# A two-layer fp32 trunk on one core: left operands two products ahead in the value stage, row scaling on ScalarE, reloads in pieces, another share of projection and output steps

## The chip, the cores and the metric

The kernel runs on one core of one Trainium2 chip. The metric is the device time of one execution in microseconds, lower being better. TensorE (PE) multiplies; VectorE (DVE), ScalarE (ACT) and GpSimd (POOL) work on tiles of 128 partitions; SyncE (SP) issues the DMAs. Each engine runs its own instructions in order and waits on semaphores for the others.

## The reference, cut to what matters

```python
def reference(x, ...):                       # x: 1 x 2048 x 1024, float32
    h = rms_norm(x, a_norm_g[0])             # layer 0: chunked gMLP
    x = x + gmlp_mixer(h, a_w_in[0], ...)
    k_pad, v_pad = shared_kv(x, kv_norm_g, w_kv)   # rms_norm(x) @ w_kv, once
    h = rms_norm(x, b_norm_g[0])             # layer 1: band attention
    x = x + chunk_attention_mixer(h, k_pad, v_pad, b_w_qz[0], b_rel_bias[0], b_w_out[0])
    return rms_norm(x, final_norm_g)
```

The attention has 16 heads of 64 channels. Each chunk of 64 rows attends to itself and the eight chunks before it, with a relative-position bias, and the result is gated by silu(z) before the output projection. All of it is float32.

## The kernel before, in words

Float32 accuracy comes from three matmuls: each operand is split into a rounded high part and the rest (hi, lo), and `mm3` (lines 113 to 115) adds hi by hi, hi by lo and lo by hi into one PSUM bank. A split is a cast on ACT followed by a subtraction on DVE. The large matrix products use a form of Strassen's scheme: seven products of half-size blocks in place of eight, the sums of blocks being formed on POOL and DVE. The 2048 rows go in four row tiles t of 512, each of four blocks b of 128 rows.

The kernel has three stages. The first, to about 1349 us of the span, is the gMLP layer; it leaves x in DRAM (`x1d`). The second is the **value stage** (the `with` block from line 1085), to 1549 us. The third is attention with its projections and the output projection.

The value stage computes v = rms_norm(x) @ w_v with `strassen("vp{t}", ...)` for each t. There are 14 products per t: the phases `PHS = (1, 7, 2, 6, 5, 4, 3)`, each for two row halves jp. Each product is four steps k of `mm3`, 12 matmuls of 128x512. `strassen` is a generator that yields after every step, so that other work can be put between. At step k = 1 of product i it calls `ready(i + 1)`, which splits the left operand of the next product: `split_s` casts into Shv on ACT (line 269) and subtracts into Slv on DVE (line 270); the tiles are in a ring "S" of eight buffers. `left` then forms the next block sums on POOL in place (lines 1112 to 1117). At the same point `weigh` calls `right` for a phase to come, with `look` saying how far: at t = 0 this loads and splits that phase's weights (line 186 on ACT, 187 on DVE). `evict` takes the finished PSUM bank (four of them): products of phases 1 and 7 are copied by ACT into vu (line 1148), the others are added by DVE (1153 to 1164), and finished parts are split again into v on ACT (1135) and DVE (1136) and stored.

Between the products of tile t the loop at the end of the stage prepares tile t + 1. At yields 1, 4, 7 and 10 `norm(t + 1, b)` loads a block of x, squares it with a row sum on ACT (line 133), takes the power -1/2 in `root` (an addition on DVE, line 126, and the power on POOL, line 127) and scales the rows on DVE (line 138). At yields 20, 28, 36 and 44 `block(t + 1, b)` transposes the block on PE (line 153), copies it back on ACT (157) and stores it (158) for later. For t = 1 and 2 the pieces of `o_sums` form block sums of the output weights on POOL, split them into tiles of the same ring "S" and store them. At t = 3, yield 20, `reload(0)` reads the four transposed blocks of tile 0 back (line 164), casts them into `hh` (167, ACT) and subtracts into `hl` (168, DVE). hh and hl have one buffer each.

The attention stage goes over t and, within it, eight head pairs p. For each pair the loop of eight u does: scores two units ahead (`score`: matmul line 1302, bias and row maximum on DVE 1310, exponential on ACT 1317, reciprocal on DVE 1320, scaling on POOL 1321), transposes of the probabilities (`flip`: PE 1341, copies on ACT 1344, split on DVE 1345) and the product with v (`value`: PE 1362 to 1369). Between them `take(gen, n)` draws steps from a generator `ahead(t, p)`, each step being three matmuls: the projection of the next pair (`project` for q and k, `gate` for z, 8 steps each, lines "pj") and then steps of the output projection of the tile before, `outs[t - 1]` ("bo"), of which `SHARE` says how many go to each pair. `steps_of` counts the steps, and they are spread evenly over 16 slots (two per u). At a **tile border** (p = 7, t < 3) the generator first calls `reload(t + 1)`, then gives 4 bo steps, then the 16 projection steps of the next tile's first pair, then 8 bo steps, spread so that 11 slots would hold them. Ahead of the loops the first pair is projected alone, and of the next pair's projection 4 steps are drawn before each of the first two scores.

## Time and profile before

| | |
|---|---|
| median of three executions | 2731.74 us (2731.46 to 2737.39) |
| the profiled execution | 2731.49 us |
| its span in the profile | 2729.7 us |
| mean granted TensorE clock | 0.987 |
| start of the value stage's matmuls | 1350.0 us |
| start of the attention stage | 1549.0 us |
| busy ACT / POOL | 49% / 33% of the span |

How to read it: the profile is one execution, and all positions are microseconds from the start of its span. "Busy" is the share in which an engine ran an instruction; the granted clock is the TensorE clock that the throttle gave, as a share of full speed. A row of the timeline has start, duration, engine, line of the kernel, operation and operands; brackets hold the idle time of that engine just before it and what ended it. A row of the waits has the engine, the waiting line, the engine or DMA that it waited for, total us, number of times and the longest.

### The profile page before, as it was taken

Reading aid. Unit: us, or ns where it says so; the run is one execution under the profiler, and the core shown is the slowest. Engines: PE = TensorE matmul, PEld = TensorE weight load, DVE = VectorE, ACT = ScalarE, POOL = GpSimd, SP = SyncE. Lnnn points to the kernel's source line nnn. Section 1 sums busy time; section 2 is a strip of 40 time slices with the busy share of each in tenths; the row PEclk is TensorE's granted clock in tenths of the full one; section 3 lists DMA queues with packets and bytes.
Section 4 is the critical chain, followed back from the end, with each engine's and each line's share of the span. In section 5 each row is a group of like instructions: output and inputs, shape, how many; then the busy total and the mean of one; then the engine's idle time right before and its main releaser. Section 6 shows DMA issues by size and latency. Waiting matters only on the chain. (4 is left out here: it accounts for less than half of the span.)

```text
span 2729.7 us, 38869 instructions
## 1 busy us (share of the span) xinstructions
PE 2629.2 (96%) x13216; PEld 2199.6 (81%) x13216; DVE 1970.0 (72%) x3097; ACT 1327.0 (49%) x2360; POOL 907.7 (33%) x906
## 2 busy tenths in 40 slices
PE   8999999999999999999989899899999999999997
PEld 7788888888888888888867677788887888788875
DVE  5655676676666668667677777777778778877787
ACT  5422242433434345332455455656656566656553
POOL 3512226142351314114234444323232223323243
PEclk9999999999999999999989999999999999999999
DMA  8898999989989879678668778766777667866677
GB/s 299 309 332 335 348 353 327 332 299 352 333 301 310 286 269 345 224 244 318 236 221 283 250 249 256 253 207 196 231 247 256 204 220 229 272 197 193 187 227 248
DMA packets 274774, 735.57 MB, mean 269 GB/s; under 512 B 29584, under 2 KB 61328, under 8 KB 274576
## 3 DMA queue, kind: packets, MB, share of 16 engines
q1 hardware_dynamic: 274576, 733.09, 78.3%
q8 instruction: 105, 1.72, 0.2%
q14 instruction: 93, 0.76, 0.1%
HBM read 540.56 MB, written 181.93 MB: 265 GB/s over the span
## 5 line engine op out<-in xcount | busy, mean ns | idle before, releaser
L113 PE MATMUL P<-T,S 128*128 128x512 f32 x1248 | 495.0, 397 | 2.1 <-ACT S L360 2.1
L115 PE MATMUL P<-T,S 128*128 128x512 f32 x1248 | 489.4, 392 | 0.0
L114 PE MATMUL P<-T,S 128*128 128x512 f32 x1248 | 488.1, 391 | 1.1 <-DVE T L363 1.1
L1321 POOL TENSOR_SCALAR pr<-pr,sl 128x640 f32<-128x640 f32 (+4 forms) x256 | 201.9, 789 | 548.1 <-DVE sl L1320 494.6
L113 PE MATMUL pj<-hh_b,wh_b 128*128 128x512 f32 x768 | 316.2, 412 | 6.0 <-ACT wh_b L186 4.2
L1317 ACT ACTIVATE pr<-pr,nm 128x640 f32<-128x640 f32 (+4 forms) x256 | 195.5, 764 | 229.1 <-DVE nm L1310 224.0
L114 PE MATMUL pj<-hl_b,wh_b 128*128 128x512 f32 x768 | 306.2, 399 | 0.0
L115 PE MATMUL pj<-hh_b,wl_b 128*128 128x512 f32 x768 | 305.6, 398 | 0.0
L115 PEld LDWEIGHTS P<-T,S 128*128 128x128 f32 x1248 | 234.8, 188 | 50.1
L113 PEld LDWEIGHTS P<-T,S 128*128 128x128 f32 x1248 | 235.2, 189 | 46.8 <-ACT S L360 2.3
L114 PEld LDWEIGHTS P<-T,S 128*128 128x128 f32 x1248 | 235.2, 188 | 46.6 <-DVE T L363 1.3
L1345 DVE TENSOR_TENSOR pt<-tp,pt 128x640 fp32r<-128x640 f32 (+4 forms) x256 | 188.7, 737 | 74.6 <-ACT pt L1344 72.5
L1310 DVE CUSTOM_DVE_ANT_0 pr<-s,bias 128x640 f32<-128x640 f32 (+4 forms) x256 | 188.1, 735 | 26.0 <-PE s L1302 20.7
L1341 PE MATMUL tp<-ident,pr 128*128 128x128 f32 x1120 | 167.0, 275 | 19.5 <-DVE pt L1345 16.9
L1341 PEld LDWEIGHTS tp<-ident,pr 128*128 128x128 f32 x1120 | 134.8, 141 | 63.2 <-issue 21.4
L1344 ACT CAST pt<-tp 128x640 fp32r<-128x640 f32 (+4 forms) x256 | 158.7, 620 | 52.7 <-PE tp L1341 49.9
L115 PEld LDWEIGHTS pj<-hh_b,wl_b 128*128 128x128 f32 x768 | 146.6, 191 | 32.7
L113 PEld LDWEIGHTS pj<-hh_b,wh_b 128*128 128x128 f32 x768 | 147.5, 192 | 25.7 <-ACT wh_b L186 5.8
L114 PEld LDWEIGHTS pj<-hl_b,wh_b 128*128 128x128 f32 x768 | 147.3, 192 | 16.9
L187 DVE TENSOR_TENSOR wl_b<-raw_b,wh_b 128x1024 fp32r<-128x1024 f32 x96 | 126.6, 1320 | 29.1 <-ACT wh_b L186 28.0
L1369 PE MATMUL pv<-pt,V 128*128 128x256 f32 x960 | 142.4, 288 | 0.9 <-ACT pt L1344 0.9
L1369 PEld LDWEIGHTS pv<-pt,V 128*128 128x128 f32 x960 | 127.0, 193 | 3.1 <-ACT pt L1344 1.8
(291 smaller groups left out, 5952.6 us busy)
## 6 DMA issues: line engine op xcount, KB each, us to landing
S<-hsd SPq DMA_DIRECT2D x288, 512.0 KB, 5.5
rw<-in_w_a SPq DMA_DIRECT2D x108, 512.0 KB, 6.4
A<-ytd SPq DMA_DIRECT2D x72, 512.0 KB, 5.8
raw_b<-wk SPq DMA_DIRECT2D x72, 512.0 KB, 3.9
hsd<-S SPq DMA_DIRECT2D x56, 512.0 KB, 4.4
V<-vhd SPq DMA_DIRECT2D x56, 512.0 KB, 4.7
wh_bo<-ows SPq DMA_DIRECT2D x50, 512.0 KB, 4.4
wl_bo<-ows SPq DMA_DIRECT2D x50, 512.0 KB, 5.6
```

The source lines that it names most:

```text
L113: mm(ps, lh, rh, start=first, stop=False)
L114: mm(ps, lh, rl, start=False, stop=False)
L115: mm(ps, ll, rh, start=False, stop=last)
L187: tv(wl[:], raw[:], wh[:].bitcast(F32), op=sub)
L1310: nc.vector.tensor_tensor_reduce(out=pr[:, c0:].rearrange("p (a b) -> p a b", a=nseg), in0=ps[:, :nseg, :w], in1=bias[:, c0:].rearrange("p ...
L1317: nc.scalar.activation(pr[:, c0:], pr[:, c0:], AF.Exp, scale=-1.0, bias=nm[:], accum_out=sl[:])
L1321: nc.gpsimd.tensor_scalar(pr[:, c0:], pr[:, c0:], sl[:], 1.0, op0=ALU.mult, op1=ALU.mult)
L1341: tpose(tp[:, b, :], pr[:, b * P : (b + 1) * P], ident[:])
L1344: nc.scalar.copy(oh, tp[:, b0:5, :])
L1345: nc.vector.tensor_tensor(pt[:, 1, b0 + qq : 5 + qq, cs], tp[:, b0:5, :], oh.bitcast(F32), op=ALU.subtract)
L1369: mm(po[:, 0, :], keys(i), pt[:, j, i, :], start=(t == 0 and j == 0 and i == blocks[0]), stop=(j == 1 and i == blocks[-1]),)
```

## The change

The change does six things.

- `norm` scales the rows with ScalarE for t = 1 to 3; t = 0 stays on VectorE.
- `strassen` has a new argument `ahead`, the number of products by which left operands are split ahead: 2 in the value stage, 1 in the output projection. In the value stage `look` is 1 for every t, and the weights of phase 2 are loaded and split by `v_weights(2)` ahead of tile 0's products.
- `reload` returns a function of the block. At t = 3 of the value stage the four pieces come at yields 20, 25, 30 and 35; at the borders pieces 0 and 1 come at u = 0 and pieces 2 and 3 at u = 1, ahead of that u's first steps.
- `SHARE` is (2, 7, 7, 7, 7, 7, 7, 12) for every t; before it was (2, 8, 8, 9, 9, 8, 8, 4) for t = 1 and 2 (t = 0 uses none).
- At the borders of t = 1 and 2, 8 bo steps stand ahead of the 16 projection steps and 4 behind them. A new `due` spreads the steps there: two bo steps in each of the first four slots, then 17/8 steps per slot; at t = 0 nothing in the first four slots.
- Ahead of each of the first two scores 6 steps are drawn, not 4.

```diff
--- before.py
+++ after.py
@@ -135,7 +135,10 @@
             accum_out=r[:],
         )
         root(r[:])
-        nc.vector.tensor_scalar(xt[:], xt[:], r[:], None, op0=ALU.mult)
+        if t:
+            nc.scalar.mul(xt[:], xt[:], r[:])
+        else:
+            nc.vector.tensor_scalar(xt[:], xt[:], r[:], None, op0=ALU.mult)
 
     def x_tiles(t):
         th = sh.tile([P, KD, T], F32R, tag="hh", name=f"hh_b{t}")
@@ -159,13 +162,16 @@
 
     def reload(t):
         th, tl = x_tiles(t)
-        for b in range(TB):
+
+        def one(b):
             xt = sh.tile([P, D], F32, tag="raw", name=f"xr_b{t}_{b}", bufs=4)
             nc.sync.dma_start(xt[:], xtd[t][b][:])
             x3 = xt[:].rearrange("p (k c) -> p k c", k=KD)
             oh = th[:, :, b * P : (b + 1) * P]
             nc.scalar.copy(oh, x3)
             tv(tl[:, :, b * P : (b + 1) * P], x3, oh.bitcast(F32), op=sub)
+
+        return one
 
     def scaled(raw, gain):
         k = gain.shape[1]
@@ -231,7 +237,7 @@
 
     PHS = (1, 7, 2, 6, 5, 4, 3)
 
-    def strassen(name, right, left, evict, look):
+    def strassen(name, right, left, evict, look, ahead):
 
         todo = [(ph, jp) for ph in PHS for jp in range(2)]
         rts, views = {}, {}
@@ -246,7 +252,8 @@
                 views[i] = left(*todo[i])
 
         weigh(1)
-        ready(0)
+        for i in range(ahead):
+            ready(i)
         for i, (ph, jp) in enumerate(todo):
             ps = pmm.tile([P, 512], F32, tag="mm", name=f"{name}_{ph}_{jp}")
             vs = views.pop(i)
@@ -256,7 +263,7 @@
                 mm3(ps[:], *vs[k], hi[:, c], lo[:, c], k == 0, k == 3)
                 if k == 1:
                     weigh(i // 2 + (2 if jp else 1 + look))
-                    ready(i + 1)
+                    ready(i + ahead)
                 if k < 3:
                     yield
             evict(ph, jp, ps[:])
@@ -1088,15 +1095,18 @@
             for q in range(2):
                 vw[ph, q] = [vp.tile([P, 1024], F32R, name=f"vw{i}{ph}_{q}")[:] for i in "hl"]
 
+        def v_weights(ph):
+            for q in range(2):
+                if ph in (6, 5):
+                    vw[ph, q] = [w_tile(f"vw{i}{ph}_{q}")[:] for i in "hl"]
+                raw = vp.tile([P, 1024], F32, tag="st", name=f"st{ph}_{q}", bufs=4)
+                nc.sync.dma_start(raw[:], vwf[ph, q][:])
+                split_in(raw, *vw[ph, q])
+
         def v_right(t):
             def right(ph):
-                if t == 0 and ph not in (1, 7):
-                    for q in range(2):
-                        if ph in (6, 5):
-                            vw[ph, q] = [w_tile(f"vw{i}{ph}_{q}")[:] for i in "hl"]
-                        raw = vp.tile([P, 1024], F32, tag="st", name=f"st{ph}_{q}", bufs=4)
-                        nc.sync.dma_start(raw[:], vwf[ph, q][:])
-                        split_in(raw, *vw[ph, q])
+                if t == 0 and ph not in (1, 7, 2):
+                    v_weights(ph)
                 return [vw[ph, q] for q in range(2)]
             return right
 
@@ -1170,15 +1180,19 @@
             vp.tile([P, D], F32, tag="xo", name=f"xo_b{t}_{b}", bufs=4) if t % 2 else even(t, b)
         )
         for t in range(NT):
+            if t == 0:
+                v_weights(2)
             for i, _ in enumerate(
-                strassen(f"vp{t}", v_right(t), v_left(t), v_evict(t), 1 if t else 2)
+                strassen(f"vp{t}", v_right(t), v_left(t), v_evict(t), 1, 2)
             ):
                 if t + 1 < NT and i in (1, 4, 7, 10):
                     norm(t + 1, i // 3, v_junk)
                 if t + 1 < NT and i in (20, 28, 36, 44):
                     block(t + 1, (i - 20) // 8)
                 if t + 1 == NT and i == 20:
-                    reload(0)
+                    again = reload(0)
+                if t + 1 == NT and i in (20, 25, 30, 35):
+                    again((i - 20) // 5)
                 if 0 < t < NT - 1 and i == 4:
                     todo = o_sums(t - 1, lambda n: v_tile("wo", n, 4), lambda n: vp.tile(
                         [P, 512], F32R, tag="S", name=n, bufs=8
@@ -1556,12 +1570,11 @@
 
         def o_all(t):
             yield from strassen(
-                f"bo{t}", o_right(t), o_left(t), o_evict(t), (t + 1) // NT
+                f"bo{t}", o_right(t), o_left(t), o_evict(t), (t + 1) // NT, 1
             )
 
         outs = [o_all(t) for t in range(NT)]
-        SHARE = {t: (2, 8, 8, 9, 9, 8, 8, 4) for t in range(NT)}
-        SHARE[NT - 1] = (2, 7, 7, 7, 7, 7, 7, 12)
+        SHARE = (2, 7, 7, 7, 7, 7, 7, 12)
 
         def take(gen, n):
             for _ in range(n):
@@ -1587,21 +1600,19 @@
                     yield from gate(t, 0)
                 yield from gate(t, p + 1)
                 if t:
-                    yield from some(outs[t - 1], SHARE[t][p])
+                    yield from some(outs[t - 1], SHARE[p])
             else:
-                if t + 1 < NT:
-                    reload(t + 1)
                 if t:
-                    yield from some(outs[t - 1], 4)
+                    yield from some(outs[t - 1], 8)
                 if t + 1 < NT:
                     yield from project(t + 1, 0)
                     values(t + 1, 0)
                 if t:
-                    yield from some(outs[t - 1], 8)
+                    yield from some(outs[t - 1], 4)
 
         def steps_of(t, p):
             n = (32 if p == 0 else 24) if p + 1 < NPAIR else (16 if t + 1 < NT else 0)
-            return n + (SHARE[t][p] if t else 0)
+            return n + (SHARE[p] if t else 0)
 
         load_bias(0, 0)
         gen = project(0, 0)
@@ -1609,16 +1620,24 @@
         values(0, 0)
         first = ahead(0, 0)
         for u in range(2):
-            take(first, 4)
+            take(first, 6)
             score(0, 0, u)
         before = None
         for t in range(NT):
             for p in range(NPAIR):
                 gen = ahead(t, p) if t + p else first
-                total = steps_of(t, p) - (0 if t + p else 8)
+                total = steps_of(t, p) - (0 if t + p else 12)
                 if t + 1 == NT and p + 1 == NPAIR:
                     last_open()
-                per = 11 if p + 1 == NPAIR and t + 1 < NT else 16
+                border = p + 1 == NPAIR and t + 1 < NT
+                if border:
+                    again = reload(t + 1)
+
+                def due(n):
+                    if not border:
+                        return total * (n + 1) // 16
+                    return (8 if t else 0) * min(n + 1, 4) // 4 + max(0, n - 3) * 17 // 8
+
                 todo = []
                 if t == 0 and p in (2, 4):
                     todo = o_sums(p // 2 + 1, lambda n: half_tile("C", n, 4), lambda n: half_tile(
@@ -1630,7 +1649,10 @@
                         score(t, p, u + 2)
                     elif p + 1 < NPAIR or t + 1 < NT:
                         score(t + (p + 1) // NPAIR, (p + 1) % NPAIR, u - 6)
-                    upto = total * (2 * u + 1) // per
+                    if border and u < 2:
+                        again(2 * u)
+                        again(2 * u + 1)
+                    upto = due(2 * u)
                     take(gen, upto - done)
                     done = max(done, upto)
                     flip(t, p, u)
@@ -1643,7 +1665,7 @@
                             value(t, p, *divmod(u // 2 - 1, 2))
                         elif before:
                             value(*before, 1, 1)
-                    upto = total * (2 * u + 2) // per
+                    upto = due(2 * u + 1)
                     take(gen, upto - done)
                     done = max(done, upto)
                 if t + 1 < NT or p + 1 < NPAIR:
```

## The prediction, written before the changed kernel was run

> **What bounds the kernel now.** I read the page's busy shares first, then busy time by window, then TensorE's own timeline with the releasers of its idle time, and last the engines that it waits for.
>
> ```profile
> span 2729.7 us, 38869 instructions
> ...
> PE 2629.2 (96%) x13216; PEld 2199.6 (81%) x13216; DVE 1970.0 (72%) x3097; ACT 1327.0 (49%) x2360; POOL 907.7 (33%) x906
> ```
>
> TensorE is busy 96% of the span, and the change takes no matmul away. So only its idle time, 2729.7 - 2629.2 = 100.5 us, and the time at a lower granted clock can be won. The windows by stage show how much of that lies where the change works. The columns are window, length, PE, PEld, DVE, ACT and POOL busy with counts, granted clock, DMA share and GB/s. Four rows are the row tiles t = 0 to 3 of the value stage, the fifth is the start of attention, three are the tile borders.
>
> ```profile
> 1348.80:1404.00 55.20, 46.21 (x200) 37.50 (x201) 44.44 (x60) 35.72 (x65) 24.39 (x19) 0.91 0.73 258
> 1404.00:1452.40 48.40, 43.83 (x201) 35.78 (x200) 34.01 (x55) 26.14 (x55) 20.46 (x17) 0.96 0.80 271
> 1452.40:1502.20 49.80, 43.48 (x202) 34.42 (x201) 38.28 (x58) 26.48 (x55) 23.36 (x19) 1.00 0.77 259
> 1502.20:1549.00 46.80, 41.17 (x170) 33.56 (x169) 39.75 (x48) 21.35 (x39) 21.37 (x12) 0.93 0.66 227
> 1549.00:1572.00 23.00, 18.65 (x74) 15.09 (x73) 8.74 (x16) 7.58 (x14) 6.45 (x7) 0.85 0.93 298
> 1762.00:1776.00 14.00, 9.95 (x47) 7.47 (x46) 11.95 (x24) 9.85 (x21) 2.92 (x9) 0.90 0.61 195
> 2058.00:2075.00 17.00, 12.58 (x60) 10.13 (x59) 14.25 (x28) 7.24 (x16) 9.52 (x11) 0.80 0.87 286
> 2354.00:2370.00 16.00, 12.17 (x60) 10.13 (x59) 13.44 (x27) 7.45 (x14) 9.22 (x9) 0.79 0.86 290
> ```
>
> What a tile would take without a stall comes from TensorE's timeline (start, duration, line; idle time before it and its releaser in brackets).
>
> ```profile
> 1360.64 0.39 PE L114 MATMUL vp<-vw,Shv 128*128 128x512 f32 x1
> ...
> 1364.07 0.39 PE L114 MATMUL vp<-vwl,Shv 128*128 128x512 f32 x1
> ...
> 1367.09 1.93 PE L153 MATMUL tr_b<-ident,xo_b 128*128 128x128 f32 x8 [2.31 <-DVE rr_b L126]
> ...
> 1375.39 1.04 PE L153 MATMUL tr_b<-ident,xo_b 128*128 128x128 f32 x8
> 1376.18 0.47 PE L113 MATMUL vp<-vwh,Shv 128*128 128x512 f32 x1
> ...
> 1387.13 0.79 PE L115 MATMUL vp<-vwh,Slv 128*128 128x512 f32 x1 [5.46 <-DVE Slv L270]
> ...
> 1418.45 0.80 PE L113 MATMUL vp<-vwh,Shv 128*128 128x512 f32 x1 [3.38 <-ACT Shv L269]
> ...
> 1477.70 0.50 PE L115 MATMUL vp<-vwh,Slv 128*128 128x512 f32 x1 [2.49 <-DVE Slv L270]
> ...
> 1524.98 0.80 PE L115 MATMUL vp<-vwh,Slv 128*128 128x512 f32 x1 [5.63 <-DVE Slv L270]
> ```
>
> The first two rows are 15 matmuls apart: (1364.07 - 1360.64) / 15 = 0.229 us each. A row tile has 14 products of 12, 168 matmuls, 38.4 us; eight transposes take 1376.18 - 1375.39 = 0.79, and four such blocks for t = 0 to 2 make 41.6 us. Against the windows the tiles lose 13.6, 6.8, 8.2 and 8.4 us, 37 in all: 25.5 idle (the windows' lengths less PE's), the rest at half clock. The big stalls wait for a left operand (Shv, Slv). One product lasts 12 x 0.229 = 2.75 us, and that is all the lead a split one product ahead has. The attention start and the borders are idle 4.35, 4.05, 4.42 and 3.83 us; their clock of 0.85, 0.90, 0.80 and 0.79 is 2 x (1 - clock) x length = 6.9, 2.8, 6.8 and 6.7 us at half speed, half of it lost: some 7, 5, 7 and 7 us each.
>
> **The change, part by part.** Times are worked from the instruction order of both kernels, with this trace's durations.
>
> *Splits two products ahead.* This adds no instruction; each split gets a lead of 5.5 us instead of 2.75. The ring S has eight buffers, and three products in flight hold six. What made the two largest waits is in DVE's and ACT's rows:
>
> ```profile
> 1383.43 1.97 DVE L187 TENSOR_TENSOR vwl<-st,vwh 128x1024 fp32r<-128x1024 f32 x1
> 1385.33 2.35 DVE L270 TENSOR_TENSOR Slv<-bx_b,Shv 128x512 fp32r<-128x512 f32 x2
> ```
> ```profile
> 1514.47 2.35 DVE L168 TENSOR_TENSOR hl_b<-xr_b,hh_b 128x1024 fp32r<-128x1024 f32 x2
> ...
> 1518.47 4.15 DVE L1136 TENSOR_TENSOR v<-vc,v 128x256 fp32r<-128x256 f32 x2
> 1522.55 2.38 DVE L270 TENSOR_TENSOR Slv<-xo_b,Shv 128x512 fp32r<-128x512 f32 x1
> ```
> ```profile
> 1417.78 0.62 ACT L269 CAST Shv<-xo_b 128x512 fp32r<-128x512 f32 x1 [4.34 <-DMA ows<-so_1h]
> ```
>
> At t = 0 (first pair of rows) the split stood behind DVE's weight splits, at t = 3 (second) behind the four hl pieces and a slow v. At t = 1 (last row) ACT's cast waited for a ring buffer that a store still read; in the changed order the cast that reuses it belongs to product 5, not 4, one product more of slack.
>
> *Row scaling on ScalarE*, 12 instructions (t = 1 to 3). DVE's and ACT's rows of like size, and POOL's ahead of the power:
>
> ```profile
> 1366.19 0.75 DVE L138 TENSOR_SCALAR xo_b<-xo_b,rr_b 128x1024 f32<-128x1024 f32 x1 [1.89 <-POOL rr_b L127]
> ```
> ```profile
> 1359.49 1.06 ACT L133 ACTIVATE jk_b<-xo_b 128x1024 bf16<-128x1024 f32 x1
> ```
> ```profile
> 1361.53 2.15 POOL L1117 TENSOR_TENSOR bx_b<-bx_b 128x512 f32<-128x512 f32 x1 [0.70 <-DVE Slv L270]
> 1364.38 1.27 POOL L1117 TENSOR_TENSOR bx_b<-bx_b 128x512 f32<-128x512 f32 x1 [0.69 <-DVE rr_b L126]
> 1365.61 0.55 POOL L127 TENSOR_TENSOR rr_b<-rr_b,mhalf 128x1 f32<-128x1 f32 x1
> ```
>
> DVE sheds 12 x 0.75 = 9 us. Scaling on ACT isn't in the trace: between 0.75 (DVE's) and 1.25 us (the Square with its read of the sum), I take 1.06. ACT, busy 65% in the first window, has room; what costs is its order. The scaling waits for POOL's power, and behind it on ACT stand the evictions vu, weight casts and the next Shv; TensorE waits for those. At t = 0 the first power still ends at 1366.2, behind the operand sums. So the first transposes still wait (2.7 instead of 2.31): scalings and the two Squares between them then fill ACT to 1372.4, two evictions and a weight cast follow to 1374.3, and Shv and Slv of product 6 end at 1374.9 and 1376.2, while TensorE wants them at 1372.2: a new stall of 4 us, with half a clock window, takes the place of the 5.46. I count **t = 0: -3.3**. At t = 1 the powers of blocks 2 and 3 stand behind the output-weight sums; stalls of 1.5 and 3 us and 1.7 us of clock replace 3.38 + 1.19 + 1.7: **-1**. At t = 2 two powers come ahead of the sums; of the 8.2 lost, 3.4 stay: **-4.8**.
>
> The Trainium skill, "ScalarE: Activation LUTs", Rules for kernel authors, says multiplications belong on VectorE and not on ScalarE. The two rows agree on price (0.75 against 1.06), yet 12 x 0.31 = 3.7 us are hidden by ACT's idle time; by the rule as price alone the sum would be 3.7 us smaller, by its order it is a rival below.
>
> *Reload in pieces at t = 3.* Four hh and hl move from one knot to four places five steps apart. Neither added nor removed: 4 loads on SP, 4 casts (1.05), 4 subtractions (1.2). With 5.5 us of lead, one hl and a slow v no longer reach TensorE; 0.9 of 8.4 stays: **-7.5**. Phase 2's weights come one step earlier; they hide behind products 0 to 3: 0.
>
> *First scores.* TensorE's row there:
>
> ```profile
> 1567.32 0.45 PE L1302 MATMUL s<-K,Qh 128*128 128x128 f32 x1 [4.35 <-DMA Qh<-Qh]
> ```
>
> Four more steps of three matmuls (0.69 each) precede the two scores, two of them ahead of the first: 1.4 us of this wait, perhaps a clock window. Nothing is computed less, and 4 steps are missing as filler later. Bounds 0 and -6; I take **-2**.
>
> *Borders.* At t = 0 the reload was the wait:
>
> ```profile
> 1769.46 3.87 ACT L167 CAST hh_b<-xr_b 128x1024 fp32r<-128x1024 f32 x4
> ```
> ```profile
> 1771.01 4.64 DVE L168 TENSOR_TENSOR hl_b<-xr_b,hh_b 128x1024 fp32r<-128x1024 f32 x4
> ```
> ```profile
> 1773.39 0.80 PE L113 MATMUL pj<-hh_b,wh_b 128*128 128x512 f32 x1 [1.79 <-ACT hh_b L167]
> ...
> 2065.63 0.56 PE L1302 MATMUL s<-K,Qh 128*128 128x320 f32 x2 [2.40 <-DVE nm L1310]
> ...
> 2068.50 0.79 PE L113 MATMUL pj<-hh_b,wh_b 128*128 128x512 f32 x1 [2.02 <-ACT wh_b L186]
> ```
>
> There is no output product to fill with at t = 0, and two pieces come one pair of slots later: hh and hl complete some 1.5 us later, **+1** (0 to +2.5). At t = 1 and 2, eight output steps (24 x 0.229 = 5.5 us) now lie ahead of the first projection, so its weights and hh have that long to come; of some 7 us I leave 1.9 of idle time and 1 of clock: **-4 each, -8**. Pairs 1 to 6 give up one or two output steps of 0.69 us: the same matmuls elsewhere, 0. Their waits bound it:
>
> ```profile
> PE tp L1341 <- DVE pt L1345: 16.9, 22, 2.4
> ...
> PE s L1302 <- DVE nm L1310: 8.7, 9, 2.4
> ```
>
> 25.6 us over 24 pairs is about 1 us each; if the twelve pairs with less filler wait a third longer, or the moved steps shorten others, that is 4 us either way.
>
> **Clock.** A gap costs beyond itself:
>
> ```profile
> 1360.00:1370.00 10.00, 7.69 (x32) 6.15 (x31) 6.78 (x10) 10.00 (x18) 5.87 (x6) 0.86 0.55 215
> ```
>
> After the gap of 2.31 us the granted clock in these ten microseconds is 0.86, so 2.8 us ran at half speed; I therefore charge about 1.7 us to gaps of two or more. The Trainium skill, "TensorE: Matmul & The Clock Gate", What's actually happening, has the clock fall after at least one idle window of about 3.4 us; by that the shorter gaps that I leave would be free, some 5 us more gain. The row differs, and it decides.
>
> **Sum.** -3.3 - 1 - 4.8 - 7.5 = -16.6 in the value stage; -2 + 1 - 8 = -9 after it; -25.6. The profiled execution took 2731.49 us (its span and 1.8 around it), a quarter of a microsecond from the median 2731.74. 2731.49 - 25.6 = 2705.9, said as **2706**. Its own range is 2697 to 2716: down, the start's other 4, the pairs' 4 and a border at 0 instead of +1 make 9 us; up, the start's 2, the border's 1.5, the pairs' 4 and scalings at 1.25 instead of 1.06 (12 x 0.19 = 2.3) make 10.
>
> **Rivals.**
>
> 1. *ScalarE's order eats t = 0 to 2.* The stall merely moves from the split to the scaling's wait. For: the in-order chain above, with 4 us left at t = 0. Against: two products of lead. The 9.1 us there are not won: 2706 + 9 = 2715.
> 2. *Nearly all goes.* If the evictions have buffers enough and the casts slip past, value -28 of 37, borders -13, start -5: 2685. Against: rr_b and the ring waits remain.
> 3. *It does not do what it says.* The waits are released by what stood behind them (weights, powers, stores) and every stall comes back elsewhere: 2731.
> 4. *Slower.* POOL sets the pace of ScalarE. If at each of t = 0 to 2 the first power waits for all eight operand sums, four at 2.15 and four at 1.27 us, that is 13.7 us; less 5.5 of lead it is 8.2, and 1.7 of clock, 9.9 each, 30 in all, while t = 3 and the rest still give 16.5: 2731.5 + 13 = 2745. It decides from a wait of 5.5 us on. Against: the trace has one sum right ahead of the first power at t = 0. The Trainium skill, "ScalarE: Activation LUTs", Rules for kernel authors, would leave the scaling on VectorE, where ScalarE can't wait for it.
>
> **How the numbers follow.** Forecast 0.54, rivals 1 to 4: 0.18, 0.10, 0.08, 0.10. A measurement of this kernel tells from no change about 0.2%, 5.5 us. Faster: 0.54 + 0.18 + 0.10 = 0.82; within: 0.08; slower: 0.10. The range leaves out rivals 2 and 4 (0.20) and reaches from 2692, the forecast's low end less 5 us in case three of the stalls that I leave cost no clock at 1.7 each, to 2733 for rival 3 with a little noise.
>
> **What would show it.** Right: TensorE's wait before the first Slv of t = 3 under 1 us and the tile near 39 us; t = 2 near 45; at t = 0 a wait of 2 to 3 us at the first transposes and one of about 4 at product 6, released by ScalarE; the borders of t = 1 and 2 with under 2 us of idle time. Wrong: a wait over 5 us on Shv at any t, vu evictions late enough that PSUM stops TensorE, a border of t = 0 longer by more than 3 us, or pairs of t = 1 and 2 that grow by more than half a microsecond each.

## The result, and the profile after

| | before | changed |
|---|---|---|
| median of 20 executions | 2730.57 us (2726.17 to 2738.24) | 2737.49 us (2727.51 to 2744.70) |
| ratio, with its 95% interval | | 1.0022 [1.0013, 1.0031] |
| span of the profiled execution | 2729.7 us | 2735.3 us |

The change makes the kernel slower by some 6 us; the forecast was 25.6 us faster. Single executions of one kernel lie up to 18 us apart, so below totals are compared by ratios with intervals, and where profiles differ on the length of a stretch, the text says so.

The page of the changed kernel, first part:

```profile
span 2735.3 us, 38862 instructions
...
PE 2634.6 (96%) x13216; PEld 2199.5 (80%) x13216; DVE 1965.0 (72%) x3085; ACT 1335.4 (49%) x2372; POOL 900.2 (33%) x906
```

VectorE has 5 us less and ScalarE 8 us more, the way the moved scaling points; TensorE's share is the same. Busy time by window, each stretch from its first matmul to the first of the next (tiles 0 to 3 of the value stage, the attention start, the pair of the border of t = 0, pair 4 of t = 1, the border pair of t = 1). The prediction's row of tile 0 begins 1.2 us ahead of its first matmul, and its rows of the borders are parts of these pairs, so they aren't set beside each other:

```profile
1351.30:1402.90 51.60, 46.19 (x201) 36.51 (x202) 37.98 (x51) 36.68 (x63) 19.27 (x15) 0.93 0.78 282
1402.90:1455.50 52.60, 44.86 (x201) 35.66 (x200) 36.08 (x58) 35.89 (x68) 25.20 (x22) 0.97 0.68 240
1455.50:1505.90 50.40, 45.70 (x202) 36.70 (x201) 34.36 (x51) 27.54 (x55) 21.56 (x17) 0.93 0.73 256
1505.90:1551.50 45.60, 40.63 (x169) 32.88 (x168) 40.67 (x48) 21.24 (x39) 24.34 (x13) 0.93 0.67 232
1551.50:1576.20 24.70, 22.30 (x92) 17.91 (x92) 12.93 (x21) 9.91 (x17) 5.26 (x9) 0.93 0.93 294
1771.20:1805.00 33.80, 28.30 (x138) 22.56 (x138) 25.99 (x52) 20.51 (x43) 10.06 (x16) 0.90 0.59 186
1943.85:1982.05 38.20, 36.60 (x209) 31.21 (x208) 29.38 (x54) 23.10 (x43) 10.77 (x15) 1.00 0.69 213
2055.90:2097.50 41.60, 38.14 (x206) 31.34 (x205) 38.78 (x71) 27.29 (x49) 14.37 (x17) 0.96 0.87 294
```

The value stage takes 200.2 us in place of 199.0. Counted from first matmuls, tile 0 gains 2.4 (it took 54.0), tile 1 loses 4.2, tile 2 loses 0.6, tile 3 gains 1.1. The stalls did not go; they have other places and other releasers. TensorE's waits in the value stage (waiting line, releaser, us in total, times, longest), before and then changed:

```profile
PE vp L115 <- DVE Slv L270: 16.3, 5, 5.6
PE vp L113 <- ACT Shv L269: 6.7, 4, 3.4
PE tr_b L153 <- DVE rr_b L126: 2.3, 1, 2.3
```

```profile
PE vp L113 <- ACT Shv L276: 12.6, 7, 2.5
PE vp L115 <- DVE Slv L277: 7.5, 6, 4.4
PE tr_b L156 <- ACT xo_b L139: 2.6, 1, 2.6
```

Before, VectorE's subtraction Slv was the larger part; now ScalarE's cast Shv is. ScalarE's four scalings at t = 1 show one reason:

```profile
1407.72 1.16 ACT L139 ACTIVATE bx_b<-bx_b,rr_b 128x1024 f32<-128x1024 f32 x1 [2.65 <-POOL rr_b L127]
...
1410.93 1.15 ACT L139 ACTIVATE bx_b<-bx_b,rr_b 128x1024 f32<-128x1024 f32 x1 [1.45 <-POOL rr_b L127]
...
1416.83 1.15 ACT L139 ACTIVATE bx_b<-bx_b,rr_b 128x1024 f32<-128x1024 f32 x1 [1.11 <-POOL rr_b L127]
...
1421.86 1.15 ACT L139 ACTIVATE bx_b<-bx_b,rr_b 128x1024 f32<-128x1024 f32 x1 [1.85 <-POOL rr_b L127]
```

Each stands in ScalarE's queue until GpSimd has its power: 7.06 us together, with Shv casts and evictions behind them. At t = 3 the one big stall is still there, 4.38 us, only later. VectorE, then GpSimd, at that place:

```profile
1537.86 0.68 DVE L1163 TENSOR_TENSOR vc<-vp,vu 128x512 f32<-128x512 f32 x1
1538.46 0.67 DVE L1166 TENSOR_TENSOR vu<-vp,vu 128x512 f32<-128x512 f32 x1
1539.06 2.95 DVE L1146 TENSOR_TENSOR v<-vc,v 128x256 fp32r<-128x256 f32 x2
1541.93 2.38 DVE L277 TENSOR_TENSOR Slv<-xo_b,Shv 128x512 fp32r<-128x512 f32 x1
...
1545.43 0.76 DVE L1146 TENSOR_TENSOR v<-vc,v 128x256 fp32r<-128x256 f32 x2
```
```profile
1536.99 2.70 POOL L179 TENSOR_TENSOR raw_b<-raw_b,bg 128x1024 f32<-128x1024 f32 x1
1539.65 2.07 POOL L179 TENSOR_TENSOR raw_b<-raw_b,kg 128x1024 f32<-128x1024 f32 x1
1541.69 2.07 POOL L179 TENSOR_TENSOR raw_b<-raw_b,bg 128x1024 f32<-128x1024 f32 x1
```

GpSimd scales three projection weights back to back, to 1543.76. Under it, v takes 2.95 us where the same pair takes 0.76 just after, and Slv takes 2.38. The two operations ahead, which read one operand from PSUM, keep their 0.68 and 0.67. The kernel before has the same picture at its own stall (the 4.15 and 2.38 us that the prediction quotes):

```profile
1518.24 2.07 POOL L173 TENSOR_TENSOR raw_b<-raw_b,bg 128x1024 f32<-128x1024 f32 x1 [5.96 <-DMA raw_b<-in_w_kqz]
1520.31 2.04 POOL L173 TENSOR_TENSOR raw_b<-raw_b,kg 128x1024 f32<-128x1024 f32 x1
1522.31 2.07 POOL L173 TENSOR_TENSOR raw_b<-raw_b,bg 128x1024 f32<-128x1024 f32 x1
```

It is so in the whole value stage of before: of its 56 Slv the 36 that no GpSimd operation overlaps take 0.67 to 0.69 us, the other 20 from 0.68 to 2.38, half of them over 1.2; VectorE's additions from PSUM stay at 0.67 to 0.69 either way. The prediction named the four hl and "a slow v" and did not ask why v was slow.

### The profile page after: what moved, and what is told of

The parts are those of the page before. It is cut to its first block, busy times and chain, and to the rows that moved or that the text cites. A ratio compares the mean times of both kernels' runs of the same rounds, so it can differ in the third digit from the quotient of the medians.

```text
span 2735.3 us, 38862 instructions
## 1 busy us (share of the span) xinstructions
PE 2634.6 (96%) x13216; PEld 2199.5 (80%) x13216; DVE 1965.0 (72%) x3085; ACT 1335.4 (49%) x2372; POOL 900.2 (33%) x906
## 4 chain that ended last, share of the span: by engine, by line
PE 76%; DVE 9%; DMA 6%; ACT 3%; issue 3%; POOL 2%; SPq 0%; DVEq 0%; POOLq 0%; ACTq 0%
PE P L115 10%; PE P L114 10%; PE P L113 10%; PE pj L113 5%; PE pj L114 5%; PE pj L115 5%; PE Po L114 4%; PE Po L115 4%; PE Po L113 4%; PE s L1316 4%; PE tp L1355 3%; PE pv L1383 3%; DMA raw_b<-in_w_kqz 1%; PE ty L768 1%; DVE Slv L277 1%
## 5 line engine op out<-in xcount | busy, mean ns | idle before, releaser
L1355 PEld LDWEIGHTS tp<-ident,pr 128*128 128x128 f32 x1120 | 135.8, 141 | 68.3 <-POOL pr L1335 20.5
L193 DVE TENSOR_TENSOR wl_b<-raw_b,wh_b 128x1024 fp32r<-128x1024 f32 x96 | 124.9, 1302 | 45.9 <-ACT wh_b L192 45.2
L192 ACT CAST wh_b<-raw_b 128x1024 fp32r<-128x1024 f32 x96 | 100.6, 1048 | 73.5 <-issue 30.2
```

The lines of the kernel that those rows point to most:

```text
L193: tv(wl[:], raw[:], wh[:].bitcast(F32), op=sub)
L1355: tpose(tp[:, b, :], pr[:, b * P : (b + 1) * P], ident[:])
```

## The experiments

Each kernel was timed beside the kernel before on the same chip; a ratio is to that. Each change is an edit of the changed kernel or of the one before. A stretch of a profile is the distance between first matmuls.

**Which half is slow.** Two kernels each hold one half of the change; two undo one part of the value stage.

e3: the value stage of before, the attention stage as changed. e4: the reverse.

```diff
# e3, against the changed kernel
-                strassen(f"vp{t}", v_right(t), v_left(t), v_evict(t), 1, 2)
+                strassen(f"vp{t}", v_right(t), v_left(t), v_evict(t), 1 if t else 2, 1)
...
-            if t == 0:
-                v_weights(2)
...
-            nc.scalar.mul(xt[:], xt[:], r[:])
...
+        nc.vector.tensor_scalar(xt[:], xt[:], r[:], None, op0=ALU.mult)
...
-                if t + 1 == NT and i in (20, 25, 30, 35):
-                    again((i - 20) // 5)
+                    for b in range(TB):
+                        again(b)
```

> The value stage as before (one ahead, scaling on VectorE, reload at one place), the attention stage as changed. Theory S with a border at t = 0 that is 3 us dearer: the total is 3 to 4 us over the kernel before. Rival A: the total is 6 us or more over it. My prediction's own terms for this part (-9) would give 9 us under it.

```diff
# e4, against the changed kernel
-        SHARE = (2, 7, 7, 7, 7, 7, 7, 12)
+        SHARE = {t: (2, 8, 8, 9, 9, 8, 8, 4) for t in range(NT)}
+        SHARE[NT - 1] = (2, 7, 7, 7, 7, 7, 7, 12)
...
-                    return (8 if t else 0) * min(n + 1, 4) // 4 + max(0, n - 3) * 17 // 8
+                    return total * (n + 1) // (11 if border else 16)
...
-            take(first, 6)
+            take(first, 4)
```

(with the reload and the order 4, 16, 8 of before)

> The value stage as changed, the attention stage as before. Theory S: 0 to 3 us over the kernel before, with ScalarE's waits for the power at t = 1 and a value stage of 199 to 202 us. Rival A: at or under the kernel before (-2 or less). My prediction's own terms for this part (-16.6) would give 17 us under it.

Measured: e3 2739.55 us, 1.0021 [1.0010, 1.0032]; e4 2733.19 us, 1.0002 [0.9993, 1.0011]. So the attention order by itself costs 5.7 us (2.7 to 8.7), and the value stage as changed is worth nothing either way. Both rule out the prediction's terms, -9 and -16.6. Theory S and rival A are not told apart by them: e3 lies between the two, and e4 fits S in the total, though its value stage takes 197.0 us and not 199 to 202.

e1: row scaling back on VectorE. e2: one product ahead.

```diff
# e1, against the changed kernel
-        if t:
-            nc.scalar.mul(xt[:], xt[:], r[:])
-        else:
-            nc.vector.tensor_scalar(xt[:], xt[:], r[:], None, op0=ALU.mult)
+        nc.vector.tensor_scalar(xt[:], xt[:], r[:], None, op0=ALU.mult)
```

> The changed kernel with the row scaling back on VectorE for every tile; all else as changed. Theory S (ScalarE stands in order at the scaling's wait for GpSimd's power, 7.1 us at t = 1, and the splits behind it come late): the value stage falls from 200.2 to about 194 us, t = 1 from 52.6 to 47, and the total is 6 us under the changed kernel. Rival A (the loss is all in the attention stage's order): t = 1 and 2 change by under 1.5 us each and the total stays within 2 us of the changed kernel. Rival V (VectorE's load was the limit): the stage becomes longer than 202 us.

```diff
# e2, against the changed kernel
-                strassen(f"vp{t}", v_right(t), v_left(t), v_evict(t), 1, 2)
+                strassen(f"vp{t}", v_right(t), v_left(t), v_evict(t), 1, 1)
```

> The changed kernel with left operands split one product ahead in the value stage; scaling on ScalarE stays. Theory S: with half the lead the wait for the power reaches TensorE in full at t = 0 to 2, some 3 us more each, total 8 us over the changed kernel. Rival L (the lead of two is itself worth nothing, since what delays a split delays it at either distance): value stage within 2 us of 200.2, total within 2 us of the changed kernel.

Measured: e1 2740.66 us, 1.0026 [1.0017, 1.0035]; e2 2741.80 us, 1.0027 [1.0011, 1.0043]. Both intervals overlap that of the changed kernel. Theory S missed in the total of both; for e2 rival L holds (value stage 199.2 us). In e1's profile tiles 0 to 2 take 149.7 us against 154.6, so the wait in order is real, but nothing of it can be told in the time, and tile 1 falls to 50.6 us only, not to 47.

**Which part of the attention order.** e5 adds the two steps ahead of the first scores to the kernel before; e16 adds the new border of t = 0; e17 the new shares and order at t = 1 and 2. e6 and e7 take the latter two out of e3.

```diff
# e5, against the kernel before
-            take(first, 4)
+            take(first, 6)
...
-                total = steps_of(t, p) - (0 if t + p else 8)
+                total = steps_of(t, p) - (0 if t + p else 12)
```

> The kernel before, with six steps in place of four drawn ahead of each of the first two scores, and nothing else. My term: -2 us. Rival (the wait for the half of Q that goes round by DMA moves, and the steps are missing as filler in the next pairs): within 2 us of the kernel before, the stretch from the first projection to the second pair at 48 to 51 us.

```diff
# e6, against e3: the border of t = 0 as before
+                    if t == 0:
+                        return total * (n + 1) // 11
...
-                    if border and u < 2:
-                        again(2 * u)
-                        again(2 * u + 1)
+                    if border and u < 2:
+                        if t:
+                            again(2 * u)
+                            again(2 * u + 1)
+                        elif u == 0:
+                            for b in range(TB):
+                                again(b)
```

> The value stage as before and the attention stage as changed, except that at the border of t = 0 the four pieces come at once and the steps are spread over 11 slots, as before. Theory B0 (that border costs 3.1 us by itself, since hh and hl end 10 us after the last gate matmul in place of 8): the pair that holds it falls from 33.9 to 30.8 us and the total to 2.6 us over the kernel before. Rival (the 3 us come back in the next pair): total unchanged against the attention stage alone, 5.7 us over.

```diff
# e7, against e3: shares, order and pace at t > 0 as before
-        SHARE = (2, 7, 7, 7, 7, 7, 7, 12)
+        SHARE = {t: (2, 8, 8, 9, 9, 8, 8, 4) for t in range(NT)}
...
+                    if t:
+                        return total * (n + 1) // 11
```

> The value stage as before and the attention stage as changed, except that the output steps' shares, the order 4, 16, 8 at the borders of t = 1 and 2 and their pace over 11 slots are as before. Theory R (eight output steps ahead of the projection don't shorten those borders, while the pairs that gave steps up wait more; 2.6 us together): total 3.1 us over the kernel before, what is left being the border of t = 0. Rival (my term, -8 from these borders): taking them back makes the total 8 us more than the attention stage alone, 14 us over the kernel before.

e16 is e7 with the first scores and the reload of t = 1 and 2 as before too; e17 is e6 with the first scores and every reload as before.

```diff
# e16, against e7
-            take(first, 6)
+            take(first, 4)
...
-                    if border and u < 2:
-                        again(2 * u)
-                        again(2 * u + 1)
+                    if border and u < 2:
+                        if t == 0:
+                            again(2 * u)
+                            again(2 * u + 1)
+                        elif u == 0:
+                            for b in range(TB):
+                                again(b)
```

> The kernel before with only the border of t = 0 as changed: two pieces at u = 0, two at u = 1, no projection step in the first four slots. Theory B0: that pair takes 33.9 us in place of 30.8, total 3 us over the kernel before. Rival (paid back by the pair behind it): total within 1 us.

```diff
# e17, against e6
-            take(first, 6)
+            take(first, 4)
...
+                    if border and u == 0:
+                        for b in range(TB):
+                            again(b)
```

> The kernel before with only the changed shares, the order 8, 16, 4 and the new pace at the borders of t = 1 and 2; their reload at one place, the border of t = 0 and the first scores as before. Theory R: 2 to 4 us over the kernel before, none of it as idle time of those borders, which keep a wait of 2 us for hh. My term: 8 us under it.

Measured: e5 2732.11 us, 1.0003 [0.9994, 1.0011]; e6 2738.95 us, 1.0018 [1.0008, 1.0028]; e7 2735.56 us, 1.0008 [0.9996, 1.0020]; e16 2735.48 us, 1.0001 [0.9991, 1.0010]; e17 2736.64 us, 1.0014 [1.0002, 1.0027]. The shares and their order are the part that costs: 3.8 us alone, as theory R has it, and without them 2.2 of the 5.7 are left; the prediction's term, by which e7 would be 14 us over the kernel before, is ruled out. e5 is worth nothing, as its rival says. The border of t = 0 does lengthen its pair (33.4 in e16, 33.8 in the changed kernel, 30.8 before), but the total of e16 doesn't show it; in its profile the four pairs behind take 143.0 in place of 143.9. e6 is not told apart from e3, and its interval holds both of its theories.

**What held VectorE.** e8: the changed kernel with the weights of the first two pairs scaled on VectorE. e10: the same edit in the kernel before. e9: in the changed value stage with the old attention order; e11: e9 with the row scaling on VectorE.

```diff
-    def scaled(raw, gain):
-        nc.gpsimd.tensor_tensor(r3, r3, gain..., op=ALU.mult)
+    def scaled(raw, gain, eng=None):
+        (eng or nc.gpsimd).tensor_tensor(r3, r3, gain..., op=ALU.mult)
-            scaled(raw, (bg if c else kg)[:, :, :])
+            scaled(raw, (bg if c else kg)[:, :, :], nc.vector if p < 2 else None)
```

> The changed kernel, with the scaling of the first two pairs' projection weights (six operations of 128x1024 at tile 0) on VectorE in place of GpSimd. Theory K (the stall of 4.4 us before Slv at t = 3 is three GpSimd scalings back to back, under which VectorE's v and Slv take 2.9 and 2.4 us instead of 0.75 and 0.68): the stall goes, t = 3 falls from 45.7 to 40 us, the total is 5 us under the changed kernel. Rival Q (VectorE's queue is what is late, its own load): VectorE has 1.2 us more for each scaling, the stall stays at 4 us or grows, total the same or over.

> The value stage as changed, the attention stage as before, and the projection weights of the first two pairs at tile 0 scaled on VectorE in place of GpSimd. Theory K (those scalings alone made the stall at t = 3, and the attention order alone made the changed kernel slower): t = 3 at 38 to 39 us with no idle time, total 7 us under the kernel before (2725). Rival: the gain of the weights' move was tied to the changed attention order; total within 2 us of the kernel before.

> The kernel before with only the weights' scaling of the first two pairs on VectorE: one product ahead, all four hh and hl at one place. Theory K alone: t = 3 falls from 46.8 to 40 us, total 6 us under the kernel before. Theory J (the lead of two and the pieces matter once GpSimd is out of the way, since the four hl of 4.8 us still stand before Slv): t = 3 stays at 43 us or more, total 2 to 3 us under it.

> As the one with the changed value stage and the weights' scaling on VectorE, but with the row scaling back on VectorE too. Theory S (ScalarE's wait in order for the power costs some 3 us at t = 0 to 2): those tiles fall from about 151 to 147 us and the total by 4. Rival N (it is nothing: VectorE's 9 us more cancel it): the three tiles and the total within 2 us.

Measured: e8 2731.28 us, 0.9994 [0.9983, 1.0005]; e9 2726.43 us, 0.9973 [0.9960, 0.9985]; e10 2723.84 us, 0.9964 [0.9951, 0.9978]; e11 2725.35 us, 0.9976 [0.9961, 0.9990]. Theory K holds in e8, e9 and e10. Against the changed kernel, e8 is 7.6 us faster, and its tile 3 has no stall at all (TensorE busy 38.00 of 38.00 us):

```profile
1502.10:1540.10 38.00, 38.00 (x169) 31.50 (x168) 33.75 (x47) 19.51 (x36) 12.87 (x8) 1.00 0.72 235
```

With one ahead and hh and hl at one place (e10), tile 3 is 40.7. So of the 8.7 us between 46.8 and 38.1, 6.1 are GpSimd's scalings alone; the other 2.6 are the pieces and not the lead, since e14 below has one ahead and the pieces and takes 38.1 too. In the total e10 is no slower than e9, which has the changed value stage besides. In e11 tiles 0 to 2 take 149.8 us against 152.8 in e9, 3 of the 4 us that theory S expects there, but their totals are not told apart.

**GpSimd's sums at t = 0 to 2.** e12: e9 with the sums of the left operands on VectorE too. e13: both moves to VectorE in the kernel before, with nothing of the change. e14: e12 one ahead. e19: e12 with row scaling on VectorE.

```diff
-                    tg(a11, a11, a21, op=sub)
-                    tg(a21, a21, a22, op=add)
+                    tv(a11, a11, a21, op=sub)
+                    tv(a21, a21, a22, op=add)
...
```

> As the one with the changed value stage and the weights' scaling on VectorE, and the sums of the left operands on VectorE in place of GpSimd (eight of 128x512 for each tile). Theory G (GpSimd's sums hold up VectorE's splits, 1.8 us for an Slv in place of 0.68, and the powers queue behind the sums): t = 0 to 2 fall from about 151 to 143 us, total 8 us lower. Rival D (VectorE, 34 to 44 of some 50 us busy, is then the limit): t = 0 to 2 at 151 us or over, total the same or higher.

> The kernel before (one product ahead, row scaling on VectorE, hh and hl at one place) with the first two pairs' weight scaling and the left operands' sums on VectorE. Theory G alone (GpSimd beside VectorE made the stalls; the lead, the pieces and ScalarE's scaling are worth nothing beside it): value stage 177 us as with the changed stage, total 2712. Theory L2 (once GpSimd is away the lead of two and the lighter VectorE show): value stage 183 us or more, total 6 us over 2712 or more.

> The changed value stage with weights and operand sums on VectorE (attention as before), but splits one product ahead. Theory L2: t = 0 to 2 rise from 139 to 144 us or more, total 5 us over the version with two ahead (2712). Rival (the lead is still worth nothing): within 2 us of it.

> The changed value stage with sums, weights and row scaling all on VectorE, attention as before: it differs from the kernel before with VectorE's sums and weights by the lead of two, the pieces and the look alone. Theory L2 (the lead is worth something once GpSimd is away): value stage 172 us or less against 176.5, total 4 us under 2707. Rival (the lead is worth nothing at either place): value stage 175 to 179, total within 3 us of 2707.

| | ahead | row scaling | hh and hl | t = 0 to 2, us | t = 3, us | total, us | ratio |
|---|---|---|---|---|---|---|---|
| e12 | 2 | ScalarE | pieces | 139.2 | 38.1 | 2711.59 | 0.9923 [0.9903, 0.9943] |
| e14 | 1 | ScalarE | pieces | 143.8 | 38.1 | 2716.11 | 0.9930 [0.9917, 0.9944] |
| e19 | 2 | VectorE | pieces | 135.8 | 38.1 | 2708.06 | 0.9906 [0.9891, 0.9921] |
| e13 | 1 | VectorE | at once | 135.8 | 40.7 | 2707.39 | 0.9902 [0.9883, 0.9921] |
| before | 1 | VectorE | at once | 152.2 | 46.8 | 2730.57 | 1 |

Theory G holds in the time: with GpSimd's sums gone, tiles 0 to 2 lose 13.6 us (e9 has 152.8), more than forecast. How much of it is VectorE held up beside GpSimd is not shown, for two other waits go with it: in e9 ScalarE waits 8.5 us for the sums themselves ahead of Shv and 11.5 us for the powers behind them, in e12 2.1 us (the sums, now on VectorE) and 6.6. e13 has nothing of the change and is as fast as e19, which has its lead, look and pieces: tiles 0 to 2 agree to 0.1 us, and theory L2 falls in e13 and e19. In e14 it holds for the tiles: with scaling on ScalarE, one ahead costs 4.6 us at t = 0 to 2 against two, though the totals' intervals overlap. So, by the profiles, the lead only makes good what ScalarE's scaling costs.

**How far it carries.** e18: e13 with all 24 weight scalings of tile 0 on VectorE.

```diff
-            scaled(raw, (bg if c else kg)[:, :, :], nc.vector if p < 2 else None)
+            scaled(raw, (bg if c else kg)[:, :, :], nc.vector)
```

> The kernel before with the left operands' sums and all of tile 0's projection weights (all eight pairs, not two) scaled on VectorE. Theory G carried on (GpSimd beside VectorE also costs in the pairs of tile 0, which lie at 191 to 201 us with 15 to 24 us idle): these pairs fall by 8 us or more, total 2700. Rival D (VectorE carries scores, splits and copies there, so 18 more operations of 1.2 us make it the limit): pairs as before or longer, total 2707 or over.

Measured: 2695.14 us, 0.9864 [0.9848, 0.9881], 37 us faster than before and the fastest of all. Its windows (tiles 0 to 3 of the value stage, then the seven pairs of t = 0 ahead of the border), and e13's and before's for the seven pairs:

```profile
1352.40:1399.60 47.20, 44.25 (x200) 35.95 (x201) 42.51 (x69) 34.01 (x61) 7.67 (x8) 0.96 0.87 303
1399.60:1442.50 42.90, 42.42 (x202) 34.67 (x201) 36.04 (x65) 26.61 (x56) 10.91 (x9) 1.00 0.86 301
1442.50:1487.20 44.70, 42.34 (x202) 34.69 (x201) 37.20 (x64) 25.99 (x55) 11.05 (x9) 1.00 0.83 291
1487.20:1527.90 40.70, 39.29 (x170) 31.30 (x169) 39.08 (x61) 21.03 (x40) 5.02 (x4) 1.00 0.78 267
1547.90:1732.00 184.10, 173.66 (x913) 141.97 (x913) 152.08 (x345) 116.30 (x266) 59.55 (x122) 0.99 0.85 277
```
```profile
1553.50:1752.80 199.30, 177.34 (x914) 143.96 (x913) 140.29 (x328) 115.63 (x266) 89.29 (x139) 0.97 0.79 255
```
```profile
1573.90:1768.20 194.30, 178.25 (x914) 144.28 (x914) 140.43 (x328) 115.89 (x267) 87.10 (x137) 0.97 0.81 259
```

VectorE is busy for 152 of 184 us there with 12 more than in e13, GpSimd has 30 less, and TensorE's idle time falls from 22 to 10.4 us. Theory G's time comes out and rival D falls. The path is again not separated: ScalarE's waits for the scaled weights fall from 28.7 us to 13.0, and TensorE's for the probabilities that GpSimd scales (line 1321) from 6.2 to 1.5.

## Why the prediction was wrong

**What bounds the kernel.** That TensorE waits in the value stage for left operands was right, and there was more to win than the 16.6 us forecast: e13 takes 22 us out of the stage without touching its matmuls. The cause was not. The prediction took the wait for a matter of lead; as changed, the stage gives nothing (e4), and the attention stage, forecast at -9, costs 5.7 us (e3).

**Tile 3, -7.5: the step that failed is "with 5.5 us of lead, one hl and a slow v no longer reach TensorE".** It gave -1.1. VectorE was not late by its queue of hl but by GpSimd's scalings beside it; the stall went with them to a later product. Without them the tile takes 38.1 (e8), 8.7 us less: nearly the forecast size, but 6.1 of it by another cause. The pieces were right at 2.6, the lead is worth nothing there (e14).

**Tile 0, -3.3: near.** Measured -2.4, with a wait of 2.6 us at the first transposes (2.7 forecast). The wait at product 6, for ScalarE's cast, came at 1.6 us where 4 was forecast, so the size is in part luck. (Of the 13.6 us that the prediction counts as lost in this tile, 1.2 lie ahead of its first matmul.)

**Tile 1, -1: wrong sign, +4.2.** The waits of ScalarE for the powers were seen, but as two short ones; all four scalings wait, 7.06 us. A scaling also takes 1.15 us, not 1.06. TensorE is idle 52.6 - 44.86 = 7.7 us in that tile. The four versions with the lead, ScalarE's scaling and GpSimd's sums (changed, e4, e8, e9) spend 154.6, 152.3, 151.3 and 152.8 us in tiles 0 to 2; the two that differ by scaling on VectorE (e1, e11) 149.7 and 149.8. That is some 3 us for ScalarE's order, and it uses up what the lead with its earlier weights gives, 2.4 (before: 152.2). It is not the whole of tile 1: with scaling on VectorE the tile still takes 50.6 and 50.4 us (e1, e11), and TensorE waits 4.2 and 4.0 us for one Shv, which stands on ScalarE behind a split of the output weights for which ScalarE waits 6.0 and 5.7 us. The prediction gave the stall of 3.38 us in that tile "one product more of slack"; one of that size is still there. **Tile 2, -4.8:** +0.6 in the changed kernel's profile, -2.9, -2.8 and -2.7 in those of e4, e8 and e9; a gain of half the size or so at best.

**First scores, -2:** nothing (e5, 1.0003). In the changed kernel TensorE's wait there falls from 4.35 to 2.3 us. Where that goes is not shown: the stretch from the first projection to the second pair takes 47.2 to 50.9 us in the profiles with six steps and 45.2 to 51.7 in those with four.

**Border of t = 0, +1:** the pair is 3 us longer. Two causes are in the waits of that stretch:

```profile
PE tp L1355 <- DVE pt L1359: 2.1, 1, 2.1
PE s L1316 <- DVE nm L1324: 1.4, 1, 1.4
PE pj L114 <- DVE hl_b L172: 1.1, 1, 1.1
PE pj L113 <- ACT hh_b L171: 0.6, 1, 0.6
```

The pieces delay hl, as said; the first two of them, 2.38 us, also stand ahead of pt on VectorE, which was left out. The maxima nm stand ahead of the first piece, not behind it. In the total the border is not to be told from nothing (e16).

**Borders of t = 1 and 2, -8: wrong, and this decides the sign.** The shares and the order alone cost 3.8 us [0.5, 7.4] (e17). The step that failed is "-4 each": the output steps ahead of the projection shorten nothing. In the kernel before only four of the 56 output steps are left for the border, so none of the "8 bo steps" behind the projection, of which the account of that kernel speaks, is drawn there; the change puts eight more steps into the border pair, 24 x 0.229 = 5.5 us. The rows of the border pair of t = 1 and of the pair behind it, before and then e17:

```profile
2058.55:2097.85 39.30, 34.35 (x185) 28.43 (x185) 34.25 (x65) 22.77 (x40) 12.52 (x15) 0.91 0.81 257
2097.85:2132.35 34.50, 34.50 (x202) 29.99 (x201) 26.84 (x51) 20.32 (x37) 7.78 (x13) 1.00 0.64 211
```
```profile
2055.10:2097.40 42.30, 36.15 (x204) 30.25 (x204) 39.56 (x72) 27.06 (x51) 13.14 (x17) 1.00 0.88 302
2097.40:2134.40 37.00, 35.42 (x205) 30.70 (x205) 29.78 (x55) 22.02 (x39) 12.77 (x16) 1.00 0.80 262
```

Together the two take 79.3 us in place of 73.8, all of the 5.5 us that were put in, and at t = 2 79.0 in place of 72.2, more than was put in. The border pair gains (3.0 us longer for 5.5 us of matmuls), with its clock at 1.00 in place of 0.91; but it is idle 6.2 us in place of 5.0, and the pair behind it, for which the prediction has no term, is 2.5 us longer (1.6 of them idle), and 2.2 at t = 2. In the changed kernel, with its pieces, the border pair of t = 1 is idle 3.5 us, where under 2 was forecast, and the two take 79.4 us. The waits did not go at the border; they have other releasers, before and then e17:

```profile
PE s L1302 <- DVE nm L1310: 2.9, 2, 2.4
PE pj L113 <- ACT wh_b L186: 2.0, 1, 2.0
```
```profile
PE tp L1350 <- DVE pt L1354: 4.2, 2, 2.9
PE pj L115 <- DVE wl_b L190: 1.6, 1, 1.6
```

"The same matmuls elsewhere, 0" nearly held. Pair 4 gives up two of nine steps, 1.4 us of matmuls, and takes 38.2 us in place of 37.3. The rows of before, pair 4 of t = 1 with nine steps and pair 4 of t = 3, which already had seven:

```profile
1942.95:1980.30 37.35, 36.92 (x213) 31.93 (x211) 30.20 (x55) 23.14 (x41) 12.60 (x15) 1.00 0.72 237
```
```profile
2531.30:2569.50 38.20, 36.61 (x209) 31.22 (x208) 29.39 (x54) 23.10 (x43) 10.82 (x15) 1.00 0.65 199
```

The second was in the trace before the change: with seven steps this pair is idle 1.6 us, not 0.4, and longer. But pairs 3 and 6 lose more than their steps (pair 3 takes 34.6 us in place of 36.7). Pairs 1 to 6 give up 5.5 us of matmuls at each of t = 1 and 2; seven profiles with the new order take 5.4 and 4.4 us less there, on average, than twelve with the old one (e7, which mixes them, isn't counted). The same seven take 6.5 and 6.9 us more for the border pair and the one behind it. From the end of the border of t = 0 to the end of the first pair of t = 3 they take 627.2 to 631.6 us (mean 628.8), the twelve 623.9 to 630.3 (mean 626.5). That the loss sits at the border and in the pair behind it is read from profiles; no run put those steps back singly, why that pair grows is open, and e7 leaves 2.2 us of the attention order's loss without a place that is told from noise.

**The rivals.** Rival 3 ("every stall comes back elsewhere") is what the value stage did. Rival 4 foresaw GpSimd as the pace, by way of ScalarE's queue and at 13 us; the pace was there, by way of VectorE too, and it had been there before the change. Its sign came true, though not its sum: the time was lost in the attention stage. The Trainium skill, "SBUF — State Buffer", SBUF: two separate sides, says that GpSimd and VectorE share a port pair which one instruction holds for its whole length, against VectorE's operations with two SBUF inputs among others. The rows above agree: v and Slv, with both operands in SBUF, take 2.95 and 2.38 us beside GpSimd, and vc and vu, with one in PSUM, 0.68 and 0.67. The prediction read the 4.15 us row and did not ask what ran on GpSimd at that time.

## What to carry to other kernels

When an operation on the releasing engine lasts several times its usual length, look at what the other engines do in those microseconds before you give it more lead: here a longer lead moved such a stall and did not remove it. Work that seems free because its engine is a third busy is not free if it slows the engine that releases TensorE; here 56 elementwise operations moved from GpSimd to the busier VectorE made the kernel 37 us faster. When steps are moved as filler, count the stretch that gets them together with the one behind it: here the first took less than the moved matmuls cost, and the second gave that back.

## What the runs showed of the hardware that was not expected

- GpSimd's sums of 128x512 take 1.3 to 1.8 us on average by group in the trace of before, and VectorE's subtraction of that size, with both operands in SBUF, 0.67 to 0.69 when none overlaps it and up to 2.38 beside a GpSimd operation. In e13 VectorE did the 32 sums of the value stage and six weight scalings besides, and the stage became 22 us shorter.
- Executions of one kernel differ by up to 0.7% (18 us). In the profiles the seven pairs of t = 0 take 190 to 201 us where their weights are scaled on GpSimd; the pairs of t = 1 to 3 with the same shares mostly agree within 1 us.
- Scaling 128x1024 rows by a column takes ScalarE 1.15 us, and VectorE 0.75 when nothing runs beside it.
